# RWKV-7 recurrence on one core: right-hand sides and outputs in four column groups of the array, triangular solutions in four diagonal tiles

## The chip, the cores and the metric

The kernel runs on one core of one Trainium2 chip. The metric is the device time of one execution in microseconds. Five engines work beside each other, each on its own list of instructions in order: TensorE (PE in the profile; PEld is its loading of weights), VectorE (DVE), ScalarE (ACT), GpSimd (POOL) and SyncE (SP), which here mostly issues DMAs. They wait for each other through semaphores. TensorE reads from SBUF and writes to PSUM, which has eight banks; ScalarE and VectorE fetch results from there.

## The reference

The reference is one inference step of two layers: sliding-window attention, then RWKV-7 time mixing, for a prompt of 2048 tokens (16 meta tokens ahead of it) and for eight short samples of four tokens. Model width is 1024; the second layer has 16 heads of 64. What bears on the change is its recurrence, per head:

```
def step(S, inp):
    r_t, w_t, k_t, v_t, a_t, b_t = inp
    sa = jnp.einsum('bhvk,bhk->bhv', S, a_t)
    S = S * w_t[:, :, None, :] + sa[..., None] * b_t[:, :, None, :] + v_t[..., None] * k_t[:, :, None, :]
    return S, jnp.einsum('bhvk,bhk->bhv', S, r_t)
```

The outputs `y` are then normalised per head (mean and variance over 64), scaled, given a bonus term, gated and projected out; a residual and a last RMSNorm follow.

## The kernel before

The kernel has three phases: attention, the second layer's projections, and from about 1640 us the recurrence, in which the gate, the output projection and the final norm of earlier tokens run beside it. The prompt is cut into units: one of 32 tokens (`m`, the meta tokens) and sixteen of 128 (`p`), each in chunks of 32 tokens, four to a unit, 65 in all. The samples are a unit `s` of their own.

Heads stand in pairs: `gr` (0 to 7) is a pair, `e` (0 or 1) the head within it, and `gh = gr // 4` a half of the eight pairs. Within a chunk the token-by-token rule becomes matrix work. `chain` does it in three steps, with a `yield` between them:

- *Right-hand sides (head).* For each pair and head a float32 matmul of a 128x32 block of `L` (scores, and the scaled vectors below them) with the 128x64 block of `Z` (solutions, values and state, stacked on the partitions). The results land in PSUM tile `C[gh]`, in rows 32 to 63 for e = 0 and 0 to 31 for e = 1, so two column groups of the array are used, for each half in its own bank. A ScalarE copy per half carries them to `R0s`.
- *Solutions.* `solve` multiplies by the inverse of the chunk's triangular matrix, `TT`, 32x32 per head. The operands' rows are one of four groups of 32, given by `quad(e, gh)`; results go to rows 64 to 127 of `C[gh]`, again two column groups. Four ScalarE copies put the solutions into `Z`.
- *New state.* `LS` times `Z`, 128x64 blocks, into the other half of `C[0]` and `C[1]`; four DVE products with the decay `pe` write it into the next chunk's `Z`.

`outputs` runs after every second chunk and makes `Y` of two chunks: a PSUM tile for each `e`, with rows by chunk, so that a burst uses two column groups. Both tiles are complete after the fourth chunk. `group_norm` of a unit runs during the next one and reads `Y` in two DVE reductions and two subtractions.

A float32 matmul appears as two MATMUL and two LDWEIGHTS records in the trace, so the 16 matmuls of a head are 32 records.

The triangular inverses are made two units ahead, on POOL, in `inverse`: the scores go through DRAM (`la_d`) into `LA`, some 60 short POOL instructions build `X`, and `X` goes through DRAM (`tt_d`) into `TT`. SyncE's queue issues these DMAs in its order, among the loads of `L`, `BK`, `Z`, `h` and the rest. POOL also clears `L` (L911) and takes powers for the norms (`var` L1564 to L1565, `ms` L1639 to L1641).

The order on each engine is made by a scheduler from the traced program: it places instructions by their order in the program and by an estimate of when they are ready. The main loop weaves generators into a chunk's steps with a budget: `ew` (group norm), `pe` (gate matmuls `pd`, projections `po`), `ahead` (scores and inverse of the unit after next). `tc.issue_after(x)` makes what is traced inside it come behind instruction `x` on `x`'s engine; `anchors` holds the last instructions of the chain for this.

```
rec = chain(u, ch)
with released() if i == 0 else ExitStack():
    next(rec)
run(ew[ch], 1.2)
run(pe[ch], VB.get((i, ch), (1.2, 1.9))[0])
next(rec)
run(ew[ch], 1.8)
run(pe[ch], VB.get((i, ch), (1.2, 1.9))[1])
...
next(rec, None)
```

## Time and profile before

| what | value |
|---|---|
| median of 3 runs (lowest, highest) | 2605.18 us (2594.49, 2605.62) |
| profiled execution: time, span | 2605.2 us, 2603.1 us |
| mean granted TensorE clock | 0.962 of full |
| busy PE / PEld / DVE / ACT / POOL | 2345.8 / 1630.3 / 1666.8 / 1218.3 / 1121.7 us |
| share of the span | 90 / 63 / 64 / 47 / 43 % |
| chain that ended last, by engine | PE 31%, POOL 21%, DVE 20%, DMA 11%, ACT 8%, issue 7%, SPq 3% |

In rows of the profile, `C<-Z,L 128*32 128x64 f32 x32` means: tile `C` was written from `Z` and `L`, the weights 128 rows by 32 columns, the moving operand 128 by 64, 32 records. In a line of the order of time the first two numbers are start and length in us; what stands in brackets is the engine's idle time before it and what ended it. In a line of a group, the numbers behind the bar are busy us, mean ns of one, and idle us before, with releasers. "SPq" is an instruction of SyncE's queue, here the issue of a DMA. All helpers share a line (L38 is every matmul, L44 every tensor-tensor operation), so tiles tell groups apart.

### The profile page before, as it was taken

How to read it: one execution, taken by the hardware profiler on the slowest of the kernel's cores; microseconds unless marked ns; L12 is line 12 of the kernel's file. 1: busy time of each engine (PE TensorE's matmuls, PEld its weight loads, DVE VectorE, ACT ScalarE, POOL GpSimd, SP SyncE). 2: the span in 40 equal slices, each digit the busy share in tenths (PEclk: the TensorE clock that was granted, in tenths of full speed). 3: DMA queues.
4: the chain of work that ended last, by engine and by line, in shares of the span. 5: the costliest groups of instructions: out<-in, count | busy, mean ns of one | idle time of the engine just before them, and what ended most of it. 6: DMA issues, size and time to landing. Idle time of an engine off the chain costs nothing.

```text
span 2603.1 us, 59317 instructions
## 1 busy us (share of the span) xinstructions
PE 2345.8 (90%) x23876; PEld 1630.3 (63%) x23876; DVE 1666.8 (64%) x3264; ACT 1218.3 (47%) x2994; POOL 1121.7 (43%) x1640
## 2 busy tenths in 40 slices
PE   6999999899999897999999998769889998899897
PEld 5877777777844445676667776446555555555553
DVE  6587674667748887666565655755565556555664
ACT  6676455565523334454344434344445443544432
POOL 4242122232112344433333325256777777766603
PEclk9999998999999998999999998889999999999898
DMA  8433222332447564322222227575444554454323
GB/s 201 122 106 111 64 74 70 130 98 73 156 113 235 201 224 141 107 85 86 102 93 86 83 84 191 140 190 131 116 116 125 126 128 106 121 129 124 80 56 83
DMA packets 346230, 312.88 MB, mean 120 GB/s; under 512 B 205546, under 2 KB 282218, under 8 KB 344131
## 3 DMA queue, kind: packets, MB, share of 16 engines
q1 hardware_dynamic: 344339, 305.30, 40.8%
q0 software_dynamic: 1616, 3.79, 0.6%
q8 instruction: 188, 3.08, 0.5%
q14 instruction: 87, 0.71, 0.1%
HBM read 191.15 MB, written 119.84 MB: 119 GB/s over the span
## 4 chain that ended last, share of the span: by engine, by line
PE 31%; POOL 21%; DVE 20%; DMA 11%; ACT 8%; issue 7%; SPq 3%; POOLq 0%; ACTq 0%; DVEq 0%
PE pd L38 22%; POOL X L44 6%; POOL XT L44 6%; DVE xm L47 5%; SPq L50 3%; DMA LA<-la_d 2%; DVE xpr L44 2%; PE po L38 2%; ACT ssb L41 2%; POOL var L44 2%; POOL L L911 2%; PE C L38 1%; DMA wst<-in_rwkv_w_in 1%; DMA x<-in_x_prompt 1%; PE sc L38 1%
## 5 line engine op out<-in xcount | busy, mean ns | idle before, releaser
L38 PEld LDWEIGHTS <-yp 128*128 128x128 f16 x1488 | 140.4, 99 | 168.1 <-issue 12.3
L47 DVE SCALAR_TENSOR_TENSOR xm<-dx,mu,xn 128x256 f32<-128x256 f32 (+2 forms) x432 | 200.3, 523 | 48.3 <-POOL dx L44 47.1
L44 POOL TENSOR_TENSOR XT<-LA,X 128x126 f32<-128x126 f32 (+24 forms) x458 | 199.1, 435 | 33.7
L44 POOL TENSOR_TENSOR X<-X,XT 128x126 f32<-128x126 f32 (+24 forms) x458 | 199.0, 435 | 32.8
L38 PE MATMUL pd<-wg,xg 128*128 128x512 f16 (+1 forms) x816 | 199.8, 391 | 0.0
L38 PE MATMUL pd<-xp,wq 128*128 128x256 f16 (+2 forms) x1728 | 186.3, 266 | 13.9 <-DVE qp L47 8.9
L38 PE MATMUL pd<-xp,wg 128*128 128x256 f16 (+2 forms) x1728 | 188.7, 271 | 1.2 <-DVE xp L44 0.8
L38 PE MATMUL po<-wo,yp 128*128 128x512 f16 x768 | 187.5, 387 | 0.6 <-DVE yp L47 0.6
L38 PE MATMUL pd<-wvv,xpr 128*128 128x512 f16 (+1 forms) x816 | 186.9, 386 | 0.0
L38 PE MATMUL pd<-xpr,w 128*128 128x256 f16 (+2 forms) x1728 | 186.3, 267 | 0.0
L44 POOL TENSOR_TENSOR ssb<-ssb,bias 128x512 f32<-128x512 f32 x64 | 86.3, 1354 | 221.8 <-DVE ssb L462 178.3
L38 PEld LDWEIGHTS <-wq 128*128 128x128 f16 x1728 | 159.4, 99 | 35.6 <-DVE qp L47 10.4
L38 PE MATMUL pd<-xpr,wkk 128*128 128x256 f16 (+2 forms) x1728 | 179.5, 264 | 0.0
L38 PEld LDWEIGHTS <-wg 128*128 128x128 f16 x1728 | 162.2, 101 | 25.2 <-issue 4.5
L38 PEld LDWEIGHTS <-w 128*128 128x128 f16 x1728 | 157.7, 99 | 27.1 <-issue 9.7
L38 PEld LDWEIGHTS <-wkk 128*128 128x128 f16 x1728 | 158.2, 98 | 15.6 <-issue 0.4
L44 POOL TENSOR_TENSOR ps<-wst,ps 128x1024 f16<-128x1024 f32 x32 | 69.4, 2169 | 226.6 <-ACT wst L41 207.5
L38 PE MATMUL pd<-w,yp 128*128 128x512 f16 x720 | 162.3, 383 | 3.8 <-DMA yp<-y 3.8
L44 DVE TENSOR_TENSOR Z<-C,pe 64x256 f32<-64x256 f32 x256 | 107.8, 421 | 68.2 <-PE C L38 62.1
L38 PEld LDWEIGHTS <-xpr 128*128 128x128 f16 (+1 forms) x816 | 78.6, 100 | 101.8 <-issue 16.5
L44 DVE TENSOR_TENSOR L<-pz,smk 64x256 f32<-64x256 f32 x256 | 108.0, 422 | 47.8 <-ACT LAs L41 29.4
L44 DVE TENSOR_TENSOR xpr<-xm,xpr 128x512 f16<-128x512 f32 (+2 forms) x144 | 98.5, 705 | 57.3 <-ACT xpr L41 57.0
(358 smaller groups left out, 4983.4 us busy)
## 6 DMA issues: line engine op xcount, KB each, us to landing
wst<-in_rwkv_w_in SPq DMA_DIRECT2D x32, 512.0 KB
wsp<-ps SPq DMA_DIRECT2D x32, 512.0 KB
BK<-bk SPq DMA_DIRECT2D x32, 512.0 KB
L<-ar SPq DMA_DIRECT2D x64, 256.0 KB
x<-in_x_prompt SPq DMA_DIRECT2D x29, 512.0 KB
xn<-xn SPq DMA_DIRECT2D x14, 1028.0 KB
ar<-aro SPq DMA_DIRECT2D x28, 512.0 KB
bk<-bko SPq DMA_DIRECT2D x28, 512.0 KB
```

What stands on the lines that cost most here:

```text
L38: return t_.matmul(out=out, lhsT=lhsT, rhs=rhs, start=start, stop=stop, **kw).ins
L41: return s_.activation(out=out, in_=in_, func=func, **kw).ins
L44: return e.tensor_tensor(out=out, in0=in0, in1=in1, op=op).ins
L47: v_.scalar_tensor_tensor(out=out, in0=in0, scalar=scalar, in1=in1, op0=op0, op1=op1)
L50: return nc.sync.dma_start(out=out, in_=in_).ins
L911: g_.memset(L[OS[e], e], 0.0)
```

## The change

Right-hand sides of both halves go into one PSUM tile, `C[0][:, 0]`, at the rows `quad(e, gh)`, which are four column groups; the loop takes the four in turn for each of the four pairs of a half. The burst starts with (gh, e) = (1, 1), and the others are made to issue behind this first one. One ScalarE copy of 128 partitions replaces two of 64. `solve` handles both halves in one burst: the rows of the operands and of the result (`C[1][:, 0]`) are the same 32 partitions, so the four tiles lie on the array's diagonal. New states stay as they were.

Outputs are kept in a tile for each pair of chunks, `Y[x]`, with rows by head `e` and chunk, again four column groups in turn. Its first matmul is that of the later chunk, and the rest issue behind it. The tile for the second pair of chunks is now asked for after the fourth chunk. `group_norm` reduces a tile as before, and subtracts the mean in four instructions of 64 partitions that bring the rows back into order; for the samples it stays at two.

```
--- before.py
+++ after.py
@@ -1360,15 +1360,15 @@
                     for e in range(2):
                         act(u.LS[c2][cc][OS[e], e, hs, :], ps[cc * 64:cc * 64 + 64, :, e, :])
 
-        def solve(u, ch, Z, R0s, out, gh):
-
+        def solve(u, ch, Z, R0s, out):
+
+            quads = [(e, gh, slice(quad(e, gh), quad(e, gh) + 32)) for gh in range(2) for e in range(2)]
             for i in range(4):
-                for e in range(2):
-                    q = slice(quad(e, gh), quad(e, gh) + 32)
-                    m = mm(out(e)[:, i, :], u.TT[q, ch, i, :], R0s[q, i, :], True, True)
-            for e in range(2):
+                for e, gh, q in quads:
+                    m = mm(out[q, i, :], u.TT[q, ch, i, :], R0s[q, i, :], True, True)
+            for e, gh, q in quads:
                 b0 = OS[e].start
-                last = act(Z[b0:b0 + 32, e, gh * 4:gh * 4 + 4, :], out(e))
+                last = act(Z[b0:b0 + 32, e, gh * 4:gh * 4 + 4, :], out[q])
             return m, last
 
         def released():
@@ -1391,15 +1391,21 @@
         def chain(u, ch):
             Z, L, LS = u.Z[ch], u.L[ch // 2][:, :, ch % 2], u.LS[ch // 2][ch % 2]
 
+
             C = [pr.tile([P, 2, 4, 64], F32, name="C", tag=f"C{gh}", bufs=1) for gh in range(2)]
-            rows = lambda e: slice(32 * (1 - e), 32 * (1 - e) + 32)
             R0s = wp.tile([P, 4, 64], F32, name="R0s", tag="l1_1")
-            for gh in range(2):
-                for i in range(4):
-                    for e in range(2):
-                        gr = gh * 4 + i
-                        anchors["PE"] = mm(C[gh][rows(e), 0, i, :], L[:, e, gr, 0:32], Z[:, e, gr, :], True, True)
-                anchors["ACT"] = act(R0s[gh * 64:gh * 64 + 64], C[gh][0:64, 0])
+
+            head = ExitStack()
+            for i in range(4):
+                for gh in (1, 0):
+                    for e in (1, 0):
+                        gr, q0 = gh * 4 + i, quad(e, gh)
+                        m = mm(C[0][q0:q0 + 32, 0, i, :], L[:, e, gr, 0:32], Z[:, e, gr, :], True, True)
+                        if (i, gh, e) == (0, 1, 1):
+                            head.enter_context(tc.issue_after(m))
+            head.close()
+            anchors["PE"] = m
+            anchors["ACT"] = act(R0s, C[0][:, 0])
 
             if ch + 1 < u.nch:
                 Zn = new_Z(u, ch + 1)
@@ -1410,9 +1416,7 @@
             else:
                 Zn = None
             yield
-            for gh in range(2):
-                out = lambda e: C[gh][64 + 32 * (1 - e):96 + 32 * (1 - e), 0]
-                anchors["PE"], anchors["ACT"] = solve(u, ch, Z, R0s, out, gh)
+            anchors["PE"], anchors["ACT"] = solve(u, ch, Z, R0s, C[1][:, 0])
             yield
             for gh in range(2):
                 Sp = C[gh][:, 1]
@@ -1429,15 +1433,23 @@
                         anchors["DVE"] = tt(v_, Zn[ps_, e, gs], Sp[ps_], u.pe[ps_, gs, ch:ch + 1].broadcast_to([64, 4, 64]), ALU.mult)
         def outputs(u, ch):
 
+
             if ch % 2 == 0:
                 return
             if ch == 1:
-                u.Y = [pr.tile([P, KC, 64], F32, name=f"Y{e}", tag=f"Y{e}", bufs=1) for e in range(2)]
+                u.Y = []
+            x = ch // 2
+            Y = pr.tile([P, KC, 64], F32, name=f"Y{x}", tag=f"Y{x}", bufs=1)
+            u.Y.append(Y)
+            head = ExitStack()
             for gr in range(KC):
-                for e in range(2):
-                    for c_ in (ch - 1, ch):
-                        mm(u.Y[e][32 * c_:32 * c_ + 32, gr, :], u.L[c_ // 2][:, e, c_ % 2, gr, 32:64],
-                           u.Z[c_][:, e, gr, :], True, True)
+                for c_ in (ch, ch - 1):
+                    for e in range(2):
+                        q0 = 64 * e + 32 * (c_ % 2)
+                        m = mm(Y[q0:q0 + 32, gr, :], u.L[x][:, e, c_ % 2, gr, 32:64], u.Z[c_][:, e, gr, :], True, True)
+                        if (gr, c_, e) == (0, ch, 0):
+                            head.enter_context(tc.issue_after(m))
+            head.close()
 
         def sample_chain(u):
             sw = a["state_wkv"][0].rearrange("(bp b2) (g e) v k -> b2 v g bp e k", b2=2, e=2)
@@ -1491,8 +1503,7 @@
                     q0 = quad(e, gr // 4)
                     mm(RU[q0:q0 + 32, 0, gr % 4, :], L[OS[e], e, gr, 0:32], Z[OS[e], e, gr, :], True, True)
             tt(v_, R0s, R0s, RU[:, 0], ALU.add)
-            for gh in range(2):
-                solve(u, 0, Z, R0s, lambda e: RU[quad(e, gh):quad(e, gh) + 32, 1], gh)
+            solve(u, 0, Z, R0s, RU[:, 1])
             u.Y = []
             for e in range(2):
                 ps = pz.tile([P, KC, 64], F32, name="pz", tag="pz")
@@ -1552,9 +1563,15 @@
                 v_.tensor_reduce(out=mean[:n, e * 8:e * 8 + 8], in_=u.Y[e][:n], axis=AX.X, op=ALU.add)
                 yield 0.6
             v_.tensor_scalar(out=mean[:n], in0=mean[:n], scalar1=1.0 / 64, scalar2=None, op0=ALU.mult)
-            for e in range(2):
-                tt(v_, u.ytm[:n, e], u.Y[e][:n], mean[:n, e * 8:e * 8 + 8].unsqueeze(2).broadcast_to([n, 8, 64]), ALU.subtract)
-                yield 0.6
+            if u.kind == "s":
+                for e in range(2):
+                    tt(v_, u.ytm[:n, e], u.Y[e][:n], mean[:n, e * 8:e * 8 + 8].unsqueeze(2).broadcast_to([n, 8, 64]), ALU.subtract)
+            else:
+                for x in range(2):
+                    for e, ps_ in HS:
+                        tt(v_, u.ytm[64 * x:64 * x + 64, e], u.Y[x][ps_],
+                           mean[ps_, x * 8:x * 8 + 8].unsqueeze(2).broadcast_to([64, 8, 64]), ALU.subtract)
+                    yield 0.9
             for e in range(2):
                 ysq = wk.tile([P, 8, 64], F32, name="ysq", tag="ysq", bufs=SQ)
                 act(ysq[:n], u.ytm[:n, e], AF.Square)
```

## Prediction

> **What bounds the kernel now.** I read the page first, then busy time by stage, then the chain of waits in each stage, then POOL's and SyncE's order of time, and last the groups of the recurrence's matmuls. The profiled execution took 2605.2 us for a span of 2603.1 us; the median of the three runs is 2605.18, so the sum below is made against 2605.2 and needs no shift.
>
> The recurrence fills the span from 1640 to about 2510 us. The view of windows gives stretch, length, then busy us (instructions) of PE, PEld, DVE, ACT, POOL, and the granted clock:
>
> ```profile
> 1640.00:1800.00 160.00, 124.14 (x1901) 83.73 (x1902) 94.36 (x220) 67.13 (x190) 79.38 (x151) 0.88 0.64 162
> 1800.00:2428.00 628.00, 562.25 (x8226) 360.86 (x8224) 368.12 (x652) 284.04 (x768) 452.20 (x853) 0.97 0.48 120
> 2428.00:2510.00 82.00, 79.02 (x1270) 52.81 (x1270) 49.61 (x193) 41.45 (x116) 28.10 (x79) 0.95 0.33 84
> ```
>
> PE is busiest everywhere, 90% in the middle stretch. The chain of waits says otherwise there. Its shares for 1800 to 2428 and for 2428 to 2510:
>
> ```profile
> by line: POOL X L44 24.5%; POOL XT L44 23.7%; DMA LA<-la_d 10.1%; issue 8.2%; POOL L L911 5.7%; POOL var L44 5.5%; SPq L50 4.5%; POOL LA L44 3.1%; PE pd L38 2.6%; PE C L38 1.9%; DMA TT<-tt_d 1.8%; DMA la_d<-LAs 1.0%; POOL ms L44 1.0%; PE pz
> by line: PE pd L38 27.0%; PE C L38 21.9%; PE po L38 13.4%; PE pz L38 12.9%; PE Y L38 7.7%; PE pz L1460 4.5%; DVE ytm L44 2.8%; PE kt L1357 2.6%; PE yps L1609 2.0%; ACT LS L41 1.8%; issue 1.2%; ACT R0s L41 0.8%; ACT room L41 0.7%; PE ns L146
> ```
>
> So the middle is a loop of POOL, SyncE's queue and one DMA; only the last 82 us are PE's. POOL's and SyncE's order of time show one turn of that loop (a unit of four chunks):
>
> ```profile
> 2008.68 1.35 SPq L50 DMA_DIRECT2D la_d<-LAs  x2
> 2011.12 1.27 POOL L44 TENSOR_TENSOR X<-X,ln 128x512 f32<-128x512 f32 x1
> 2012.42 1.35 SPq L50 DMA_DIRECT2D tt_d<-X  x2
> 2013.86 0.64 SPq L50 DMA_DIRECT2D h<-h  x1
> 2014.60 1.12 SPq L50 DMA_DIRECT2D LA<-la_d  x2
> 2021.82 1.92 POOL L44 TENSOR_TENSOR LA<-LA,ln 128x1024 f32<-128x1024 f32 x1 [9.43 <-DMA LA<-la_d]
> 2064.19 1.27 POOL L44 TENSOR_TENSOR X<-X,ln 128x512 f32<-128x512 f32 x1
> ```
>
> An inverse ends at 2012.39; its store `tt_d` leads SyncE's queue, `h` and the next load `LA` follow, the load lands 9.43 us after the inverse's end, and the next inverse ends at 2065.46. One turn is 2064.19 − 2011.12 = 53.07 us: 9.43 of waiting and 43.6 of POOL's own order. No matmul stands in it.
>
> **The matmuls that change.** Groups over the recurrence (count, busy us, mean ns of one, idle before):
>
> ```profile
> L38 PE MATMUL C<-Z,L 128*32 128x64 f32 x2048 | 79.1, 229 | 15.8 <-DVE Z L44 9.1 <-issue 5.9 <-PE kt L1357 0.8
> L38 PE MATMUL C<-R0s,TT 32*32 32x64 f32 x2080 | 70.1, 222 | 34.1 <-DMA TT<-tt_d 24.9 <-ACT R0s L41 9.1
> L38 PE MATMUL Y<-Z,L 128*32 128x64 f32 x2048 | 65.5, 222 | 0.0
> ```
>
> One chunk issues 32 instructions for right-hand sides and 32 for solutions, two chunks 64 for outputs. At full clock their bursts are these, and ten-nanosecond windows tell how many of one kind are in flight (the number behind the second figure):
>
> ```profile
> 2024.36 1.09 PE L38 MATMUL C<-Z,L 128*32 128x64 f32 x32
> 2026.65 0.90 PE L38 MATMUL C<-R0s,TT 32*32 32x64 f32 x32
> 2013.66 0.64 PE L38 MATMUL C<-R0s,TT 32*32 32x64 f32 x16
> 2021.86 1.98 PE L38 MATMUL Y<-Z,L 128*32 128x64 f32 x64
> 2510.90:2510.91 0.01, 0.01 (x4) 0.01 (x2) 0.00 (x0) 0.00 (x0) 1.00 0.00 0
> 2024.90:2024.91 0.01, 0.01 (x8) 0.01 (x4) 0.00 (x0) 0.00 (x0) 1.00 0.64 206
> 2027.10:2027.11 0.01, 0.01 (x16) 0.01 (x6) 0.00 (x0) 0.00 (x0) 1.00 0.29 102
> ```
>
> The first window is a sample product that always writes one column group: 4 in flight at some 222 ns each, one per 55 ns. The second is a head on two column groups in turn: 8, one per 28. The third is the place in a solve where the pairs of both halves overlap, four different tiles: 16, one per 14. The rate goes with the number of tiles in turn, and no floor is seen down to 14 ns.
>
> **The change, priced.** *Heads and outputs* go from two column groups in turn to four. Bounds: 28 ns per instruction (nothing gained: each holds all 128 rows, and no row of before shows four streams through the same rows) and 14 ns. I take 14, since doubling from one to two halved the time exactly. A burst is a lead of 1.09 − 31 × 0.027 = 0.25 us plus the steps: 32 become 0.25 + 31 × 0.014 = 0.68 us, 64 become 1.13. *Solutions* come in one burst on four diagonal tiles: 0.68 against 0.90 whole or 2 × 0.64 split; here 14 ns is shown. All in all 64 heads, 65 solves and 32 output bursts take 43.5 + 44.2 + 36.2 = 124 us against 214.7 by the groups: PE sheds up to 91 us, 5.7 a unit. How much of that reaches the end is the question.
>
> The Trainium skill ("TensorE: Matmul & The Clock Gate", Part 1, the section on 56 against 53.3 ns) says that start-to-start never falls below about 25 ns however small the matmul. By that the change would give next to nothing on heads and outputs; the window with 16 in flight disagrees for four tiles, and I do not follow it.
>
> *The middle, 1800 to 2428: nothing.* The POOL loop hides it. Were that cover gone, the 5.7 us would count in each of some 12 units, −68 us.
>
> *The last 82 us.* The groups of that window:
>
> ```profile
> L38 PE MATMUL C<-R0s,TT 32*32 32x64 f32 x192 | 6.9, 232 | 2.9 <-ACT R0s L41 2.9
> L38 PE MATMUL Y<-Z,L 128*32 128x64 f32 x192 | 6.7, 220 | 0.0
> L38 PE MATMUL C<-Z,L 128*32 128x64 f32 x160 | 6.4, 222 | 0.0
> ```
>
> Six solves, three outputs and five heads cost 20.0 us and would cost 4.1 + 3.4 + 3.4 = 10.9. PE is busy 79.02 of 82.00, so nearly all of the 9.1 counts: **−8**, bounds 0 and −9.1.
>
> *The start, 1640 to 1800.* PE is busy 124 of 160, and the chain is mixed:
>
> ```profile
> by line: PE pd L38 9.7%; DMA TT<-tt_d 9.2%; POOL X L44 6.8%; issue 6.0%; PE C L38 5.7%; DMA tt_d<-X 4.7%; DMA la_d<-LAs 4.7%; DVE Z L44 4.5%; DMA bont<-bo 4.4%; DMA vt<-v 4.3%; POOL XT L44 4.1%; DVE L L44 3.9%; POOL var L44 3.6%; DVE ytm L4
> ```
>
> PE's `C` bursts hold 5.7% of 160 = 9.1 us of it, a third of them state products that stay as they are; of the other 6 a bit under half goes: **−3**, bounds 0 and −6.
>
> *End of the middle.* The sample's inverse starts on a load that PE's scores hold back, not the inverse before it:
>
> ```profile
> 2369.51 1.59 PE C L38 x32
> 2372.51 0.83 PE C L38 x32
> 2387.77 9.64 DMA LA<-la_d
> ```
>
> A head at reduced clock and a solve stand in that chain: **−1.5**, bounds 0 and −2.
>
> *What is added.* One ScalarE copy per chunk goes (`R0s` for all partitions in one), off the path. The mean's subtraction becomes four DVE instructions of 64 partitions instead of two of 128; if a quarter costs what a half does (bounds: half as much, and the same), that is 1.29 us more a unit. The deviation is needed for `var` on POOL:
>
> ```profile
> 2025.89 1.29 DVE L44 TENSOR_TENSOR ytm<-Y,mean 128x512 f32<-128x512 f32 x2
> 2032.61 0.69 DVE L1561 TENSOR_REDUCE var<-ysq 128x8 f32<-128x512 f32 x1
> 2037.22 0.20 POOL L1564 TENSOR_SCALAR var<-var 128x16 f32<-128x16 f32 x1
> ```
>
> DVE's sum ends at 2033.3 and POOL takes it at 2037.22: 3.9 us to spare, so the middle hides the 1.29. The last units' normalisation has no such cover: **+1.3**, bounds 0 and +2.6. The wait moved: a head now stands behind the last of the four `Z` products on DVE and holds up all of PE behind it, where half a head could go before. No DMA is added, and none changes its queue.
>
> Sum: 2605.2 − 8 − 3 − 1.5 + 1.3 = **2594.0 us**, 0.4% faster; with the terms' bounds 2588 to 2608.
>
> **Rivals.** (1) *Four groups run no faster than two*, as for the rule above, because all four draw on the same 128 rows. Then only solves gain: 6.9 − 4.1 = 2.8 at the end, 1 at the start, less 1.3: 2602.7. For it: no row with four streams per row; against: the exact halving from one to two.
>
> (2) *The POOL loop opens.* The scheduler fixes SyncE's order by its own estimate of when things are ready. `la_d` leaves at 2008.68 + 1.35 and, by
>
> ```profile
> 2383.79 3.37 DMA la_d<-LAs
> ```
>
> takes 3.4 us, so it is there at about 2013, before `LA` goes at 2014.60. With earlier scores and `LA` ahead of `tt_d`, a turn loses 1.6 us at once (11 turns: −18, 2576). PE's own load would be 562/12 − 5.7 = 41 us a unit and its waits are (628 − 562)/12 = 5.5, so it would bind at some 47; with 4 of the 6 us in between won in 11 turns, 2594 − 44 = 2550. Against it: 11 turns all with the same order now.
>
> (3) *Slower: the overlap of the halves is lost.* Today a half head runs while DVE still makes the other half:
>
> ```profile
> 2116.44 0.64 PE L38 MATMUL C<-Z,L 128*32 128x64 f32 x16
> 2117.31 0.64 PE L38 MATMUL C<-Z,L 128*32 128x64 f32 x16 [0.23 <-DVE Z L44]
> 2116.31 0.86 DVE L44 TENSOR_TENSOR Z<-C,pe 64x256 f32<-64x256 f32 x2
> L41 ACT ACTIVATE R0s<-C 64x256 f32<-64x256 f32 x128 | 48.2, 377 | 10.4 <-PE C L38 7.5
> ```
>
> Whole heads wait 0.86 us more, and whole solves wait for the one `R0s` copy (0.38 us; two of 0.38 now, the first half's solve behind the first). Where PE has no dense matmul to put in between, a chunk loses about 1.3 us. In the middle PE has (628 − 562)/12 + 5.7 = 11 us a unit to lose before it decides; at the start and the end, some 20 chunks, it would cost 26 against the 12.5 gained: 2605.2 + 13.5 = 2619. It decides from 0.6 us of new idle time a chunk. For it: idle PE also lowers its clock, as after the 2.36 us wait here, where the clock falls to 0.57:
>
> ```profile
> 2104.13 1.72 PE L38 MATMUL pz<-L,BK 128*64 128x128 f32 x16 [2.36 <-POOL X L44]
> 2104.20:2108.20 4.00, 4.00 (x51) 3.19 (x52) 1.99 (x4) 2.11 (x7) 3.47 (x8) 0.57 0.73 177
> ```
>
> Against it: dense matmuls stand between the steps of nearly every chunk.
>
> **How the numbers follow.** Forecast 0.50, no faster groups 0.12, the loop opened 0.18, the overlap lost 0.20. The measurement tells 0.5%, 13 us, from no change, and the forecast lies just inside: of its 0.50 I give 0.23 to faster and 0.27 to same. Faster 0.23 + 0.18 = 0.41, same 0.27 + 0.12 = 0.39, slower 0.20. The likeliest case's own range is 2586 to 2603; to hold 8 in 10 it reaches half into the opened loop and to the overlap lost: 2562 to 2619.
>
> **What would show it.** Right: bursts of 32 heads near 0.68 us with 15 or 16 in flight, outputs near 1.13, POOL's turn still 52 to 53 us with `LA` behind `tt_d`, and PE's idle time in the middle up by about 5 us a unit; the end stretch some 8 us shorter. Eight in flight would show rival 1. A turn below 51 us, or `LA` ahead of `tt_d`, would show rival 2. PE waiting on `Z` or `R0s` by over 0.6 us a chunk would show rival 3. A POOL `var` that waits for DVE would show that the four subtractions are not hidden, and the middle would grow.

## The result, and the profile after

The changed kernel takes **2620.8 us** (median of 6 runs, 2616.2 to 2628.1) against 2596.9 us (6 runs, 2594.1 to 2605.6) of the kernel before in the same session: a ratio of **1.0086, 95% interval 1.0062 to 1.0110**. It is slower; 2594.0 was forecast, and the range ended at 2619.

The profiled execution after took 2616.2 us for a span of 2614.1, 11.0 more than the span before. The one before had been 8.3 us above its median and this one lies 4.6 below its own, which makes up the 23.9 between the medians.

The bursts do what was priced. The next fence has the order of time of the kernel after (start, length) and two ten-nanosecond windows in the middle of a head and of an output burst; the one behind it has the groups over the recurrence:

```profile
2018.95 0.65 PE L38 MATMUL C<-Z,L 128*32 128x64 f32 x32 [3.58 <-issue]
2023.83 0.67 PE L38 MATMUL C<-R0s,TT 32*32 32x64 f32 x32
2029.61 1.10 PE L38 MATMUL Y<-Z,L 128*32 128x64 f32 x64
2019.20:2019.21 0.01, 0.01 (x17) 0.01 (x9) 0.01 (x1) 0.00 (x0) 0.00 (x0) 1.00 1.21 205
2030.20:2030.21 0.01, 0.01 (x16) 0.01 (x9) 0.00 (x0) 0.01 (x1) 0.00 (x0) 1.00 0.06 0
```

```profile
L38 PE MATMUL C<-Z,L 128*32 128x64 f32 x2048 | 53.8, 260 | 51.2 <-issue 45.2 <-DVE Z L44 4.3 <-PE pz L38 1.6
L38 PE MATMUL C<-R0s,TT 32*32 32x64 f32 x2048 | 46.5, 227 | 13.3 <-DMA TT<-tt_d 6.8 <-ACT R0s L41 6.5
L44 DVE TENSOR_TENSOR ytm<-Y,mean 64x512 f32<-64x512 f32 x64 | 44.0, 688 | 1.4
L38 PE MATMUL Y<-Z,L 128*32 128x64 f32 x2048 | 38.2, 229 | 0.0
```

Heads take 0.65 us where they took 1.09, solutions 0.67 where they took 0.90, outputs 1.10 where they took 1.98, with 16 or 17 instructions in flight. The three groups are busy for 138.5 us against 214.7. And yet the span grew. The window of the middle and its chain of waits after:

```profile
1800.00:2428.00 628.00, 510.20 (x8068) 310.95 (x8069) 380.00 (x659) 261.91 (x718) 430.37 (x845) 0.89 0.48 119
by line: POOL X L44 27.8%; POOL XT L44 21.8%; DMA LA<-la_d 13.0%; issue 8.5%; POOL L L911 6.3%; POOL var L44 5.0%; SPq L50 3.4%; POOL LA L44 3.4%; DMA tt_d<-X 2.1%; DMA la_d<-LAs 1.4%; POOL ms L44 1.2%; PE po L38 1.1%; PE pd L38 1.0%; PE C 
```

The middle is still the loop of POOL, SyncE's queue and the load of `LA`, but that load has grown from 10.1% of the chain to 13.0%, PE is busy 52 us less in the same 628 us, and its clock falls from 0.97 to 0.89. To see where the time came in, the fourth and the thirteenth `X<-X,ln`, the last instruction of an inverse, cut the trace into a start, nine turns of the loop, and an end. Before, then after, in POOL's order of time:

```profile
1906.90 1.27 POOL L44 TENSOR_TENSOR X<-X,ln 128x512 f32<-128x512 f32 x1
2378.88 1.27 POOL L44 TENSOR_TENSOR X<-X,ln 128x512 f32<-128x512 f32 x1
```

```profile
1907.78 1.28 POOL L44 TENSOR_TENSOR X<-X,ln 128x512 f32<-128x512 f32 x1
2397.09 2.15 POOL L44 TENSOR_TENSOR X<-X,ln 128x512 f32<-128x512 f32 x1
```

Up to the fourth: +0.9 us. Nine turns: 471.98 and 489.31, **+17.3** (52.4 and 54.4 a turn). From the thirteenth to the end of the span: 224.2 and 217.0, −7.2. Sum +11.0. Most of the loss is in the nine turns, the stretch that the forecast held to be fixed. The +0.9 hides a second part, for the start holds the phases ahead of the recurrence too, which the change leaves alone. The last `rkh<-r,k` of the projections, before and after, shows that they ended 8.5 us later in the profile before:

```profile
1612.11 0.72 POOL L44 TENSOR_TENSOR rkh<-r,k 128x256 f32<-128x256 f32 x1
1603.58 0.72 POOL L44 TENSOR_TENSOR rkh<-r,k 128x256 f32<-128x256 f32 x1
```

From there to the fourth `X<-X,ln` it is 294.8 us before and 304.2 after, **+9.4**: the first comes 7.6 us sooner, but the three turns behind it take 174.0 us instead of 157.0. Two of the nine turns after, in SyncE's and POOL's order of time:

```profile
2012.85 0.33 SPq L50 DMA_DIRECT2D la_d<-LAs  x1
2015.29 1.27 POOL L44 TENSOR_TENSOR X<-X,ln 128x512 f32<-128x512 f32 x1
2016.58 1.35 SPq L50 DMA_DIRECT2D tt_d<-X  x2
2018.02 0.63 SPq L50 DMA_DIRECT2D la_d<-LAs  x1
2019.97 1.11 SPq L50 DMA_DIRECT2D TT<-tt_d  x2
2021.18 0.38 SPq L50 DMA_DIRECT2D out_y_prompt<-h  x1
2021.66 1.16 SPq L50 DMA_DIRECT2D LA<-la_d  x2
2032.34 1.92 POOL L44 TENSOR_TENSOR LA<-LA,ln 128x1024 f32<-128x1024 f32 x1 [15.27 <-DMA LA<-la_d]
2073.98 1.26 POOL L44 TENSOR_TENSOR X<-X,ln 128x512 f32<-128x512 f32 x1
2075.27 1.35 SPq L50 DMA_DIRECT2D tt_d<-X  x2
2076.72 1.28 SPq L50 DMA_DIRECT2D LA<-la_d  x2
2082.93 1.91 POOL L44 TENSOR_TENSOR LA<-LA,ln 128x1024 f32<-128x1024 f32 x1 [7.68 <-DMA LA<-la_d]
```

In the first turn the second `la_d` store stands behind `tt_d`, and `LA` behind `TT` and an output. `LA` is issued 5.1 us after the inverse's end (2016.56), and POOL waits 15.27 us for it: a turn of 58.7 us. In the next one `LA` follows `tt_d` directly, the wait is 7.68 and the turn some 49. The two kinds alternate through the nine turns (58.4, 49.1, 58.7, 49.3, 58.9, 49.7, 59.2, 49.0, 57.1); before, every turn there was 52 to 54 and every wait 8.1 to 9.9. POOL's own part, 43 to 44 before, is 41.6 to 43.4 after. No line of the diff names these DMAs; the scheduler ordered SyncE's queue anew around the shorter work.

A second trace of the change is the head that waits 3.58 us in the first row above. On DVE, and then on PE:

```profile
2017.11 1.28 DVE L47 SCALAR_TENSOR_TENSOR h<-h,ms,fg 128x1024 f32<-128x1024 f32 x1 [1.53 <-POOL ms L44]
2018.42 0.43 DVE L44 TENSOR_TENSOR Z<-C,pe 64x256 f32<-64x256 f32 x1
2021.14 2.77 PE L38 MATMUL pd<-wg,xg 128*128 128x512 f16 x6
2024.44 2.12 PE L38 MATMUL pd<-wg,xg 128*128 128x512 f16 x9
2076.76 1.08 PE L38 MATMUL C<-Z,L 128*32 128x64 f32 x32 [3.78 <-issue]
```

The last of four `Z` products stands on DVE behind the scaling of `h`, which waits for a power from POOL; the whole head starts only behind that product. After this wait six `pd` took 2.77 us where nine took 2.12 three us later, and the head of the next unit, behind a wait of 3.78, took 1.08 instead of 0.65. Over the middle the view of waits has:

```profile
PE C L38 <- issue: 36.2, 12, 4.2
```

That is 36.2 us in 12 waits, the longest of 4.2; in the kernel before it was a single wait of 5.9.

So two theories stand against each other. **S**: the loss is the place of `la_d` and `LA` on SyncE's queue. **W**: it is the wait of whole heads for the last `Z`, with the clock that falls after it, and heads and solves in four groups cost time of their own. The expectations of the first four runs call W by the letter H. P, from the sixth run on, says that POOL's own work and the wait for `LA` bind the turn, whatever PE does.

### The profile page after: what moved, and what is told of

Same layout as the page of the kernel before. It is cut to its first block, busy times and chain, and to the rows that moved or that the text cites. A ratio compares the mean times of both kernels' runs of the same rounds, so it can differ in the third digit from the quotient of the medians.

```text
span 2614.1 us, 59211 instructions
## 1 busy us (share of the span) xinstructions
PE 2275.0 (87%) x23876; PEld 1565.8 (60%) x23876; DVE 1695.0 (65%) x3296; ACT 1189.4 (45%) x2929; POOL 1112.8 (43%) x1640
## 4 chain that ended last, share of the span: by engine, by line
PE 29%; POOL 22%; DVE 20%; DMA 11%; ACT 8%; issue 7%; SPq 2%; POOLq 0%; ACTq 0%; DVEq 0%
PE pd L38 21%; POOL X L44 7%; POOL XT L44 6%; DVE xm L47 5%; DMA LA<-la_d 4%; SPq L50 2%; DVE xpr L44 2%; ACT ssb L41 2%; POOL L L911 2%; PE po L38 1%; POOL var L44 1%; DMA wst<-in_rwkv_w_in 1%; PE sc L38 1%; PE oT L38 1%; DMA x<-in_x_prompt 1%
## 5 line engine op out<-in xcount | busy, mean ns | idle before, releaser
L47 DVE SCALAR_TENSOR_TENSOR xm<-dx,mu,xn 128x256 f32<-128x256 f32 (+2 forms) x432 | 200.1, 522 | 49.3 <-POOL dx L44 48.1
L44 POOL TENSOR_TENSOR X<-X,XT 128x126 f32<-128x126 f32 (+24 forms) x458 | 207.7, 453 | 33.5
L38 PE MATMUL pd<-wg,xg 128*128 128x512 f16 (+1 forms) x816 | 213.5, 410 | 0.0
L44 POOL TENSOR_TENSOR XT<-LA,X 128x126 f32<-128x126 f32 (+24 forms) x458 | 179.7, 392 | 35.4 <-DMA Z<-v 1.5
L38 PE MATMUL pd<-xp,wg 128*128 128x256 f16 (+2 forms) x1728 | 183.0, 267 | 0.7 <-DVE qp L47 0.4
L38 PE MATMUL po<-wo,yp 128*128 128x512 f16 x768 | 181.7, 381 | 2.1 <-DVE yp L47 2.1
L38 PE MATMUL pz<-L,BK 128*64 128x128 f32 x1024 | 85.0, 320 | 106.4 <-DVE L L44 63.8
L41 ACT ACTIVATE LAs<-pz 32x128 f32<-32x128 f32 x240 | 64.3, 268 | 214.3 <-PE pz L38 211.2
L38 PEld LDWEIGHTS pz<-L,BK 128*64 128x64 f32 x1024 | 68.6, 161 | 126.9 <-POOL XT L44 76.8
```

Source lines behind the costliest of these rows:

```text
L38: return t_.matmul(out=out, lhsT=lhsT, rhs=rhs, start=start, stop=stop, **kw).ins
L41: return s_.activation(out=out, in_=in_, func=func, **kw).ins
L44: return e.tensor_tensor(out=out, in0=in0, in1=in1, op=op).ins
L47: v_.scalar_tensor_tensor(out=out, in0=in0, scalar=scalar, in1=in1, op0=op0, op1=op1)
```

## The experiments

The edits write an order into a kernel: a dependency without a semaphore makes one DMA issue behind another on the same queue. The first two and the fifth are the kernel after with the stores `tt_d` of a unit behind the next unit's last `la_d`, or behind its `LA`:

```
+    def behind(u, ins):
+        for x in stores.get(u.idx - 1, ()):
+            tc.add_manual_dep(x, ins.name, mybir.DependencyInfo(NoSync, DATA))
...
+            last = dma(LA[...], la_d...)            # or la_d's second store
+            if u.kind == 'p' and u.idx > 4:
+                behind(u, last)
...
+            stores.setdefault(u.idx, []).append(dma(tt_d..., X[...]))
```

This table holds all that follows: ratios to the kernel before in the same session, and, from one profiled execution each, the mean of the nine turns between the same two `X<-X,ln` rows.

| run | median us | ratio, 95% interval | us a turn |
|---|---|---|---|
| before, profiled | | 1 | 52.4 |
| after, profiled | 2620.8 | 1.0086 (1.0062 to 1.0110) | 54.4 |
| after, both `la_d` first | 2589.8 | 0.9971 (0.9956 to 0.9986) | 51.1 |
| after, `LA` first | 2575.9 | 0.9929 (0.9902 to 0.9956) | 50.8 |
| before, `LA` first | 2576.9 | 0.9930 (0.9908 to 0.9953) | 51.5 |
| before, `LA` late in every second unit | 2615.7 | 1.0077 (1.0060 to 1.0094) | 56.0 |
| after, order of before | 2583.1 | 0.9965 (0.9945 to 0.9984) | 51.5 |
| after, `LA` first, `h` late | 2555.5 | 0.9860 (0.9822 to 0.9898) | 48.3 |
| before, `LA` first, `h` late | 2562.0 | 0.9880 (0.9845 to 0.9914) | 50.8 |
| heads and solves, `LA` first | 2663.0 | 1.0260 (1.0221 to 1.0300) | 58.8 |
| after, `LA` first, `h` late, clearing on ScalarE | 2568.1 | 0.9895 (0.9874 to 0.9917) | 49.9 |
| before, `LA` first, `h` late, clearing on ScalarE | 2591.9 | 0.9988 (0.9972 to 1.0004) | 52.2 |
| outputs alone | 2592.4 | 0.9985 (0.9970 to 1.0001) | 52.8 |
| heads and solves alone | 2642.1 | 1.0180 (1.0151 to 1.0210) | 56.2 |
| heads and solves, order of before up to the last units | 2607.3 | 1.0053 (1.0035 to 1.0071) | 53.7 |
| outputs, order of before | 2581.4 | 0.9963 (0.9946 to 0.9980) | 51.4 |
| before, order held to the end | 2576.1 | 0.9924 (0.9905 to 0.9943) | 51.7 |
| heads and solves, order held to the end | 2584.8 | 0.9961 (0.9948 to 0.9974) | 51.9 |
| outputs, order held to the end | 2579.8 | 0.9941 (0.9921 to 0.9961) | 51.6 |
| after, order held to the end | 2580.2 | 0.9941 (0.9919 to 0.9962) | 51.7 |

**The order alone, in the kernel after and in the kernel before.** In the fourth of these the kernel before gets the order of the kernel after in every second unit:

```
+        odd = u.kind == 'p' and u.idx > 4 and u.idx % 2 == 1
...
+            with tc.issue_after(last_t[u.idx - 1]) if odd and e == 1 else ExitStack():
+                dma(la_d[e]..., u.LAs...)
...
+            with tc.issue_after(last_T[u.idx - 1]) if odd else ExitStack():
                 dma(LA[...], la_d...)
```

> The changed kernel, with one thing forced: both stores of the next unit's scores (la_d) stand ahead of the store of this unit's inverse (tt_d) in SyncE's queue, in every unit from the fifth on. Theory S (SyncE's order turned the loop from an even 52.4 us into 49 and 58.5 in turn): every turn has its load LA right behind tt_d, the wait for it is 6 to 8 us, a turn 49 to 51 us, and the time falls from 2621 to some 2580. Theory H (the halves' overlap that was lost, and PE's lower clock after its waits, cost the time): SyncE's order does not matter, 2615 to 2625.

> The changed kernel, with the load LA of the next unit forced ahead of the store tt_d of this one. Theory S: the load no longer waits for the inverse before it, the wait is 4 to 6 us, a turn 47 to 49 us, the time some 2556 to 2570. Theory H: 2615 to 2625.

> The kernel before, with the same load LA forced ahead of tt_d. Theory S: the turn of 52.4 us falls until PE binds, which by its load of 47 us and waits of 3 to 5 is at some 50 us: 2597 - 26 = 2570, and some 10 us slower than the changed kernel with the same order, since there PE has 5.7 us a unit less to do. If the four column groups are worth nothing even then, the two come out alike. Theory H: the changed kernel stays over 1% slower than this one.

> The kernel before, with the order of the changed one forced in every second unit: the second store la_d stands behind tt_d, and the load LA behind the loads TT. Nothing else differs. Theory S: those turns grow by some 6 us to about 58, six of them, and the time rises from 2597 to 2620 or 2630. Theory H: the time stays within 0.5% of 2597.

With nothing changed but the place of two stores the kernel after goes from 1.0086 to 0.9971, and the kernel before, with `LA` put late, from 1 to 1.0077. Theory H had 2615 to 2625 us for the first two runs and no change for the fourth. S's own figures were too hopeful: 2590 and 2576 us came out where it had some 2580 and 2556 to 2570, and the third run is not 10 us behind the second but equal to it. The lower clock is not the cause either: the first run's mean granted clock is 0.944, the kernel after's 0.942. SyncE's and POOL's order of time of that fourth run shows the turn of the kernel after in the kernel before:

```profile
2000.97 1.27 POOL L44 TENSOR_TENSOR X<-X,ln 128x512 f32<-128x512 f32 x1
2002.26 2.18 SPq L50 DMA_DIRECT2D tt_d<-X  x2
2008.02 1.09 SPq L50 DMA_DIRECT2D TT<-tt_d  x2
2009.21 1.21 SPq L50 DMA_DIRECT2D LA<-la_d  x2
2021.52 1.91 POOL L44 TENSOR_TENSOR LA<-LA,ln 128x1024 f32<-128x1024 f32 x1 [19.29 <-DMA L<-ar]
```

Here POOL waits 19.29 us and the turn, to the next `X<-X,ln` at 2063.86, is 62.9, longer still than in the kernel after: `LA` leaves 7.0 us after the inverse's end instead of 5.1, and the row names a load of `L`, issued behind `LA`, as what came last. In the units between, one of the two `LA` loads moved ahead of `tt_d` by itself, and those turns are of 49 us. So the order costs as much as the whole change did, without any of its matmuls. `LA` first gives the same time in both kernels, 0.993.

**The order of before in the kernel after, and the heads' wait.** The fifth run writes SyncE's order of before (`la_d`, `tt_d`, `h`, `LA`, `TT`) into the kernel after: beside `tt_d` behind `la_d`, as above, `LA` behind the load of `h`.

```
+                hl = dma(u.h1[:n], h1_d[t] ...)
+                for x in loads.get(u.idx + 3, ()) if u.kind == "p" and u.idx > 1 ... else ():
+                    tc.add_manual_dep(x, hl.name, mybir.DependencyInfo(NoSync, DATA))
```

The sixth and seventh put `LA` first, and on DVE the scaling of `h` behind the `Z` products of the last chunk:

```
+            if ch == 2 and Zn is not None and scaled_h:
+                tc.add_manual_dep(scaled_h.pop(), anchors["DVE"].name, mybir.DependencyInfo(NoSync, DATA))
```

The eighth is the kernel before with the hunks of the change in `solve`, `chain` and `sample_chain`, without those in `outputs` and `group_norm`, and with `LA` first.

> The changed kernel, with SyncE's order of the kernel before restored around the loop (la_d, tt_d, h, LA, TT in every unit from the fifth on). If the whole loss came from SyncE's order, a turn is 52 to 53 us as before and what is left is the change's own worth. By the prediction's sum (a gain of 11 us outside the middle) the time is some 2586; if the matmuls' gain is lost to new waits there too, it is 2597 to 2604, since the run with both la_d ahead had turns of 51.2 us and 2590. If SyncE's order was not the cause, some 2621.

> The changed kernel with LA ahead of tt_d, and in addition the scaling of h on DVE, which waits for POOL's power, forced behind the four Z products of the third chunk, so that the whole head no longer waits for it. Theory W (with the loop opened, PE's wait of 3.5 us before the head of a unit's last chunk, and the lower clock behind it, eat the matmuls' gain): a turn falls from 50.9 to 47 to 48 us and the time from 2576 to some 2545. Theory P (POOL's own 42 us and the 7 us of LA bind as much): a turn stays at 50 and the time within 8 us of 2576.

> The kernel before with the same two orders forced. Theory W: its half heads did not wait for h, so only the order of the loads acts: within 8 us of 2577, and by 20 to 30 us slower than the changed kernel with the same orders. Theory P: both alike.

> The kernel before with the right-hand sides and the solutions of the change alone (outputs and the mean's subtraction as before), and LA ahead of tt_d. PE sheds 3.5 of the 5.7 us a unit. If the four column groups count once the loop is opened, the time lies between 2577 and what the changed kernel gains; theory W says that the whole head's wait for h is in it too: 2575 to 2582. If the outputs' part and its four subtractions cost something, this one is faster than 2576 by 5 us or more.

The fifth, at 0.9965, looked like the forecast come true (11 us are 0.43%). That reading did not hold, as the last four runs show. The sixth beats both kernels at 2555.5 us, between the 2545 of W and the 2568 and more of P; its `LA` is on the way before `tt_d`, and PE stands on its chain again:

```profile
2042.04 1.27 POOL L44 TENSOR_TENSOR X<-X,ln 128x512 f32<-128x512 f32 x1
2044.56 1.09 SPq L50 DMA_DIRECT2D LA<-la_d  x2
2049.74 1.91 POOL L44 TENSOR_TENSOR LA<-LA,ln 128x1024 f32<-128x1024 f32 x1 [5.24 <-DMA tt_d<-X]
by line: POOL X L44 18.9%; POOL XT L44 17.7%; PE pd L38 9.4%; issue 8.0%; POOL var L44 5.0%; PE pz L38 4.4%; PE C L38 4.1%; POOL L L911 3.9%; DMA la_d<-LAs 3.9%; DMA LA<-la_d 3.7%; POOL LA L44 2.9%; DMA tt_d<-X 2.4%; PE po L38 2.0%; SPq L50
```

But the seventh gained too by the same edit (0.9930 to 0.9880, some 13 us), where W saw nothing to gain since its heads go by halves. So the late scaling is worth time in both kernels and is no proof for W; the two differ by 6.5 us with overlapping intervals. Inside the two profiles they differ more. In the seventh, the kernel before, the chain of 1800 to 2428 is no longer POOL's:

```profile
by line: PE pd L38 11.6%; issue 7.8%; PE po L38 7.4%; PE C L38 7.1%; DVE L L44 6.7%; DVE ytm L44 5.2%; DVE Z L44 4.9%; DMA vt<-v 4.1%; SPq L50 3.7%; POOL X L44 3.5%; POOL XT L44 3.5%; DMA L<-ar 3.0%; PE pz L38 2.8%; DVE h L47 2.8%; PE Y L38
```

PE is busy there for 580.88 of the 628 us, in the sixth for 547.34, and the sixth's nine turns are 22.4 us shorter (434.87 against 457.27). So in this pair, with the loop opened, PE's shorter bursts do show in the turn. The sixth gives 8.9 us back between the projections and the fourth `X<-X,ln`, and 5.8 at the end. Its first turn, which the edit does not reach yet, is alone some 17 us longer, since it waits 19.49 us for `LA` and the seventh's 1.41. What the change is worth with this order held from the start was not tried.

The eighth missed by far, and its rows say why:

```profile
2035.17 1.26 POOL L44 TENSOR_TENSOR X<-X,ln 128x512 f32<-128x512 f32 x1
2036.10 0.99 SPq L50 DMA_DIRECT2D la_d<-LAs  x2
2041.26 1.09 SPq L50 DMA_DIRECT2D LA<-la_d  x2
2042.44 1.72 SPq L50 DMA_DIRECT2D tt_d<-X  x2
PE C L38 <- DMA TT<-tt_d: 95.4, 22, 6.1
```

`la_d` stood late on the queue, `LA` had to wait for it, and `tt_d`, forced behind `LA`, left 6.0 us after the inverse's end; then PE waited 95.4 us for `TT`. An order that helps one kernel starves another, and this run says nothing about heads and solves.

**Opening the loop further.** The ninth and tenth add to the sixth and seventh that ScalarE, not POOL, clears `L`:

```
-                    g_.memset(L[OS[e], e], 0.0)
+                    for c in range(2):
+                        act(L[OS[e], e, c], zero[OS[e]].unsqueeze(2).broadcast_to([64, KC, 64]))
```

> The changed kernel with both orders forced (LA ahead of tt_d, the scaling of h behind Z), and the clearing of L moved from POOL to ScalarE from the fourth unit on, 3.9 us of POOL a unit. Theory P (POOL's 42 us and the load of 5 us bind the turn of 47.9 us): a turn falls to 44 to 45 us, the time from 2555 to some 2520. If another wait binds, it stays above 2545.

> The kernel before with the same two orders and the same move of the clearing. Theory P: here PE, with some 46 us of work a unit, stops the turn at 47 to 48 us, so the time is some 2540, and the changed kernel with the same three edits is 15 to 20 us faster: the worth of the four column groups once POOL no longer hides it. If the two come out within 6 us, PE's work is not what binds even then.

Both times missed. The tenth is slower than without the move (0.9988 against 0.9880); the ninth, 0.9895 against 0.9860 with overlapping intervals, is at best no faster. POOL's part of a turn did fall, but ScalarE became late. POOL's waits and the chain of the ninth, 1800 to 2428:

```profile
POOL ms L1675 <- ACT sq L41: 68.4, 12, 6.3
by line: PE pd L38 9.6%; PE po L38 8.7%; issue 7.7%; DMA TT<-tt_d 7.2%; PE C L38 6.9%; SPq L50 5.3%; ACT L L41 5.1%; DMA vt<-v 3.8%; DMA tt_d<-X 3.8%; DVE ytm L44 3.7%; PE pz L38 3.7%; DVE L L44 3.7%; DMA ln<-ln 3.3%; DMA L<-ar 3.1%; DMA la
```

What they do tell: with the same order on SyncE in both, and in the ninth a chain that is no longer POOL's, the kernel with four groups is 23.8 us (0.93%) ahead of the one without, 20.8 of them in the profiles' nine turns (449.36 against 470.14), where 15 to 20 were expected. That fits PE's time counting where PE is on the path; other causes of the 23.8 us were not taken apart.

**The parts, first without an order and then with one.** Outputs alone are the kernel before with the hunks in `outputs` and `group_norm`, heads and solves alone those in `solve`, `chain` and `sample_chain`.

> The kernel before with the outputs' part of the change alone (four column groups for Y, and the four subtractions). SyncE's order comes out uneven again (la_d or LA behind tt_d and TT, in a pattern of three units). Theory S: turns alternate between some 48 and 60 us, and the time lies above 2597, at 2605 to 2625. If the order does not matter, PE's 2 us a unit are hidden and the time is 2590 to 2597.

> The kernel before with the right-hand sides and the solutions alone. SyncE's order stays even (tt_d, h, LA in each unit, la_d ahead of tt_d or right behind it). Theory S: turns of 52 to 54 us and a time within 0.6% of 2597. If the whole heads' lost overlap is what costs, it is above 2612.

Both went against S as it was put: the first lies where the order was to matter nothing, the second above the 2612 us of the lost overlap. Outputs alone have an uneven order (turns of 48 to 50, 52.9 and 58 us in threes) but a mean turn of 52.8, no worse than before: the short turns repay the long ones. Heads and solves alone lose twice what both parts lose together, with turns of 52 and 59 in alternation. So the parts had to be compared with one order. The thirteenth and fourteenth write it in for the units of the middle:

> The kernel before with the heads and the solves in four groups alone (the outputs as before), and in the middle units SyncE's order of before written into it: la_d's stores of the next unit, tt_d's stores, the load of h, LA's loads, TT's load. Alone and without that order (2642.1 us, 1.018) its turns alternate between 52 and 59 us, with waits for LA of 8.6 and 16 us. Theory S (the loss lies in where LA's load stands behind tt_d's store and TT's load on SyncE): every turn is back at 51 to 53 us, no wait for LA above 11 us, the ratio between 0.995 and 1.004. Theory W (the heads and solves in four groups are slower themselves, since a whole head waits for the last product of its chunk): the ratio stays above 1.010, and the turns that are long stay so with short waits for LA.

> The kernel before with the outputs in four groups and their four subtractions alone (heads and solves as before), with SyncE's order of before written into the middle units as in the run beside it. Alone and without that order (2592.4 us, 0.9985) its turns went 48 to 50, 52.9 and 58 us in threes. Theory S: the turns are even at 51 to 53 us; the prediction's own terms for this part (the outputs of the last units and of the start, less the subtractions, some 5 us) would give 0.997 to 0.999; with the order held, the two parts' ratios multiply to that of both together with the order held, 0.9965, within 0.003. If the parts' own prices are not additive, that product is off by more.

The thirteenth falls between the bands. Where the order is held its turns are 51 to 53.6 us; three long ones (60.7, 58.7, 58.6) stand in the last units, where it is not. The fourteenth, at 0.9963 with nine turns of 50.6 to 52.4 us, is close to what was expected; but the two parts' ratios multiply to 1.0016, 0.005 from the 0.9965 of both together, where 0.003 was allowed. The last four runs hold it to the end, in the kernel before as well. The edit, in each of the same form:

```
+    def issue(u, what, ins):
+        issued.setdefault((u.idx, what), []).append(ins)
+        for first, second in (('la', 'tt'), ('h', 'L'), ('L', 'T')):
+            d = {'la': 1, 'h': -3, 'L': 1}[first]
+            pairs = [(ins, x) for x in issued.get((u.idx - d, second), ())] if what == first else \
+                    [(x, ins) for x in issued.get((u.idx + d, first), ())] if what == second else []
+            for a, b in pairs:
+                tc.add_manual_dep(b, a.name, mybir.DependencyInfo(NoSync, DATA))
```

> The kernel before with SyncE's order written in from the second full unit to the last: la_d's stores, tt_d's stores, the load of h, LA's loads, TT's load. The kernel before keeps that order by itself in nearly every unit; only its last full turn (59.7 us, a wait for LA of 16.3 us) has LA behind tt_d's store and TT's load. Theory S: that turn falls to 52 us and the ratio to 0.996 to 0.999; the other turns stay at 51 to 53 us. Without any effect of the order: 1.000.

> Heads and solves in four groups alone, with the same order to the last unit. In the run with the order held only up to the last four units three turns were still of 59 to 61 us, and the ratio 1.0053. Theory S: no turn of the middle above 54 us, and a time within 0.4% of the kernel before with its order held in the same way; the prediction's terms for the heads and solves alone (some 4 us of the 11) would put it 0.1 to 0.2% under that one. Theory W (heads and solves in four groups cost time of their own): 0.4% or more above it.

> Outputs in four groups alone, with the same order to the last unit. Theory S: turns of 51 to 52 us, 0.1 to 0.5% under the kernel before with its order held.

> Both parts, the kernel after, with the same order to the last unit. Theory S and the prediction's own sum with the order of before kept: 0.2 to 0.6% under the kernel before with its order held (the sum was 11 us, 0.43%), and the ratios of the two parts multiply to this one within 0.3%. Theory W: no gain against it, or a loss.

None of the nine turns is over 54.3 us in any of the four. The kernel before and the kernel after, both held; the same two rows and the window of the middle:

```profile
1887.74 1.27 POOL L44 TENSOR_TENSOR X<-X,ln 128x512 f32<-128x512 f32 x1
2352.59 1.27 POOL L44 TENSOR_TENSOR X<-X,ln 128x512 f32<-128x512 f32 x1
1800.00:2428.00 628.00, 575.62 (x8536) 367.65 (x8531) 386.37 (x728) 296.13 (x803) 466.30 (x915) 0.98 0.48 122
```

```profile
1893.12 1.27 POOL L44 TENSOR_TENSOR X<-X,ln 128x512 f32<-128x512 f32 x1
2358.01 1.26 POOL L44 TENSOR_TENSOR X<-X,ln 128x512 f32<-128x512 f32 x1
1800.00:2428.00 628.00, 528.80 (x8497) 324.60 (x8496) 405.64 (x752) 273.69 (x746) 470.30 (x924) 0.92 0.47 121
```

Nine turns: 464.85 and 464.89 us. PE is busy 46.8 us less, and none of it arrives. From the thirteenth `X<-X,ln` to the end of the spans (2570.6 and 2571.2): 218.0 and 213.2, −4.8. Up to the fourth: +5.4, of which 1.2 lie ahead of the recurrence. The medians are 2576.1 and 2580.2: +0.17%, and with the half-widths 0.0019 and 0.0021 taken as independent between −0.12% and +0.46%. Heads and solves alone come out 0.37% above the held kernel before (from +0.14% to +0.60% by the same reckoning), just under the 0.4% that W asked. But in their profile, 14.7 us longer, 7.5 lie ahead of the recurrence, in phases that the change leaves alone, 4.8 between there and the fourth `X<-X,ln`, 2.4 in the nine turns (467.3 against 464.9) and none in the end (218.0 in both).

As they were put, the last expectations mostly failed. The fifteenth, at 0.9924, lies below its 0.996 to 0.999. The seventeenth and the eighteenth, which S had put under the fifteenth, lie 0.17% above it, and no gain is what W had said of the eighteenth. The ratios of the parts to the held kernel before multiply to 1.0054, 0.37% off the 1.0017 of both, where 0.3% was allowed.

What follows: of the 0.86% by which the change made the kernel slower, 0.69 go when both kernels have the same order, and the 0.17 that are left can't be told from nothing. The order is the cause that these runs show for the 0.69. W is not what makes the turn, but that heads and solves alone cost something of their own, 0.37%, is not excluded. The kernel before gains from the held order too, 0.76%, as much as from `LA` first. In its two profiles, leaving out the phases ahead of the recurrence, 5.8 us of it lie ahead of the fourth `X<-X,ln`, 7.1 in the nine turns and 6.2 behind them, where the last turn falls from 59.7 to 51.3. The edit orders three pairs (`la_d` ahead of `tt_d`, `h` ahead of `LA`, `LA` ahead of `TT`) and no more: in the held kernel before `h` goes ahead of `tt_d` in about every second turn, in the held kernel after in none.

## Why the prediction was wrong

**The step that failed** is the sentence "No DMA is added, and none changes its queue", with the zero that stood for the middle behind it. Both halves of the sentence are true, but a DMA can change its place on a queue, and the sum took SyncE's order of before as given. The forecast did say that the scheduler fixes this order by its own estimate of when things are ready; shorter bursts change that estimate. Rival 2 used it only for a gain and set it aside because all 11 turns had the same order. That was misread: ten turns in a row had it. The full turn ahead of them and the one behind them had `la_d` behind `tt_d` and `LA` behind `TT`, and they took 59.1 and 59.7 us:

```profile
1812.44 1.91 POOL L44 TENSOR_TENSOR LA<-LA,ln 128x1024 f32<-128x1024 f32 x1 [15.55 <-DMA LA<-la_d]
2397.57 1.91 POOL L44 TENSOR_TENSOR LA<-LA,ln 128x1024 f32<-128x1024 f32 x1 [16.34 <-DMA LA<-la_d]
```

So the trace before already held the order that the change brought to every second turn, and its price, some 7 us a turn. Where the sum had nothing, the profiles showed +17.3 us: five turns of 57 to 59, and four of 49 to 50 that give part of it back. In the turns ahead of these nine the same order cost more, as the start shows below.

**Right: the prices of the bursts.** 0.68 forecast and 0.65 to 0.67 measured for heads and solutions, 1.13 and 1.10 for outputs, with 16 or 17 of some 229 ns in flight: 14 ns per instruction, for four streams through the same 128 rows as well. Rival 1 falls. So does, for these matmuls, the floor of about 25 ns that the Trainium skill ("TensorE: Matmul & The Clock Gate", Part 1) gives. The shed PE time was 76.2 us rather than 91. Most of the difference, 10.3 us, is in the heads, whose 2048 records ran at a mean of 260 ns instead of 229; heads such as the one of 1.08 us behind a wait, at a granted clock of 0.50, are part of it, and whether they are all of it was not counted.

**Right, but not in the kernel as built: the middle hides PE's gain.** With the order of before held in both, nine turns agree within 0.1 us, and PE's busy time falls by 46.8/12 = 3.9 us a unit where 5 to 5.7 were forecast as idle. Where the loop was opened (the sixth against the seventh, the ninth against the tenth) PE's saving shows: the turns of the changed kernel are 2.3 to 2.5 us shorter, by one profile of each.

**The end, −8 − 1.5 + 1.3 = −8.2.** The term was mis-sized. From the thirteenth `X<-X,ln` on the kernel after is 7.2 us shorter, but 7.0 of it is the last turn (59.7 before, 52.7 after), so that the work behind it gained next to nothing; with the order held in both it is −4.8, the last turn 1.4 longer and the work behind it 6.2 shorter. So between nothing and 6.2 us came of the work behind that turn, and not, as "nearly all of the 9.1 counts" had it, PE's whole saving. What took the rest was not settled.

**The start, −3.** Measured from the last `rkh<-r,k` it is +9.4, and +4.1 with the order held. As built, `LA` stands behind `TT` in the first two of the three turns, with waits of 19.66 and 19.79 us. In those first units SyncE's order still differs between the two held kernels too. By the same row the first `X<-X,ln` comes 7.9 us earlier in the held kernel after, and the next three turns are 12.1 longer, 11.2 of it in waits for `LA` (9.96, 12.33 and 9.32 us against 2.34, 10.41 and 7.66). So there too the time went into the loop of POOL and `LA`; whether the queue's order is the whole cause was not tried and stays open. So the sum of what the change is worth by itself is about nothing, where 11 us were forecast: in this pair of profiles the start gave back what the end gained.

**Four subtractions.** They take 0.688 us each, four in place of two of 1.29 together: 2.75, so 1.46 more a unit where 1.29 was priced. A quarter does cost what a half does. `var` on POOL never waits for DVE in the middle, so they are hidden as forecast.

**Rival 3** gave 2619, next to the measured 2620.8, for another reason. Its wait is there (PE's `C` waits 36.2 us in 12 times in the middle for an issue that hangs on `Z`), and PE's granted clock is lower, yet the same kernel runs at 0.9971 once two stores change place, and in that run PE's `C` waits no less for the same cause (61.3 us in 13 times). A number that fits does not show its mechanism.

## What to carry to other kernels

Where a scheduler orders a DMA queue by estimated times, a change of the compute is also a change of that order: read the queue's sequence around the loop that binds, before and after, and price a load put behind a store that it does not need. Hold the order fixed, in the kernel before too, before saying what a change is worth; here that split a loss of 0.86% into 0.69 of order and a rest that can't be told from nothing. An engine that sheds work while another loop binds gains at most at the ends of the stage; where that loop was opened, the same shed work came out as 2.3 to 2.5 us a turn in two pairs of profiles. The best kernel of this study came from opening the loop itself (the change with `LA` ahead of `tt_d` and `h` behind `Z`): 2555.5 us, 0.9860 (0.9822 to 0.9898).

## What the hardware showed unexpectedly

Two waits of PE, of 3.58 and 3.78 us, were each followed by a granted clock of 0.50, but not at the same moment. Behind the first, the head still ran at 1.00 (0.65 us), and the clock was 0.50 from 2021.14 to 2023.83 and 1.00 from 2024.40 to 2029.60: a `pd` matmul took 0.46 us and then 0.24. Behind the second it was 0.50 at once, from 2076.76 to 2081.00, and the head took 1.08 us. PE's mean granted clock fell from 0.962 to 0.942 with less work to do, and in the pair with the order held it is 0.968 before and 0.947 after. A load's place on the queue costs more than the issue times ahead of it: `LA` issued 5.1 us after the inverse's end was used 15.8 after it, `LA` issued 1.5 after it was used 7.7 after, so that 3.6 us of queue became 8.1 of delay. In the late case its source, the second `la_d`, had gone out only 3.6 us ahead of it, and `TT`'s load ran beside it; which of the two held it was not tried.
